# Gate and up of a SwiGLU half as a 2x2 block product in seven half products instead of eight

## The chip, the cores and the metric

One core of one Trainium2 chip runs the whole layer in one program. The metric is device microseconds of one execution, as the median over runs. The core has a matrix engine (TensorE, "PE" in the profile, with its weight loads shown apart as "PEld"), VectorE ("DVE"), ScalarE ("ACT"), GpSimd ("POOL") and a queue that issues the transfers from device memory ("SP"). Each engine works through its own instructions in the order in which they stand, and waits for the others through semaphores. TensorE's operands lie in SBUF; its results lie in PSUM, in banks of 128 partitions by 512 numbers.

## The reference

The layer is a SwiGLU half, a mixing stage and a second SwiGLU half, all in float32, for 512 tokens of width 1024 and a hidden width of 2816.

```python
def rms_norm(x, g, eps=RMS_EPS):
    xf = x.astype(jnp.float32)
    ms = jnp.mean(xf * xf, axis=-1, keepdims=True)
    return (xf * lax.rsqrt(ms + eps) * g.astype(jnp.float32)).astype(x.dtype)

def swiglu(x, w_gate, w_up, w_down):
    return (jax.nn.silu(x @ w_gate) * (x @ w_up)) @ w_down
...
        x = x + FFN_HALF * swiglu(rms_norm(x, norm_ffn1[l]), ffn1_gate[l], ffn1_up[l], ffn1_down[l])
        ...
        x = x + jnp.concatenate([o_sb, o_rw], axis=-1) @ w_out[l]
        x = x + FFN_HALF * swiglu(rms_norm(x, norm_ffn2[l]), ffn2_gate[l], ffn2_up[l], ffn2_down[l])
```

## The kernel before

Everything is kept transposed: a tile has 128 features in the partitions and the 512 tokens along the free axis. `X` is the layer's state in 8 such tiles. A SwiGLU half (`ffn`) runs over `NF` = 22 feature tiles of 128 hidden features. For each it forms gate and up as products over 8 k tiles (`dense`, `gemm`), then `t` = gate times the norm scale `S`, a Silu of it on ACT, `u` = up times `S`, and their product `h` on POOL. The `S` of a half is ready only after its first gate product, since the norm's weight `g` goes into the input tiles and its scale comes in behind the product. After the 22 tiles come 8 down products over all of them ("dn"), which add into `X`.

Each float32 product is made of three passes. Both operands are split into a high part `hi` (rounded to float32r) and a low part `lo` = value minus `hi`; `mm3` (lines 176 to 179) multiplies high by high, high by low and low by high. The weights are split as they arrive (`load_split`): line 162 is the rounding on ACT, line 163 the subtraction on VectorE, both of whose operands lie in SBUF:

```python
        cp(hi[:, :n], raw[:, :n])
        pool.tensor_tensor(lo[:, :n], raw[:, :n], hi[:, :n].bitcast(F32), SUB)
```

So a feature tile takes 4 weight blocks of 128 by 512, 4 roundings on ACT, 4 subtractions on VectorE, and 2 x 8 x 3 = 48 matmuls of 128x512. `h` is split in the same way (lines 189, 190) and kept for the down products. POOL has one instruction per feature tile, line 302.

A scheduler places the instructions of each engine from the program's order and from priorities; `tc.high_priority(500)` moves an instruction forward. The result is fixed at build time. Tiles of a tag share a fixed number of buffers (`NB`): a new one waits until the last reader of the one before is done.

Of the kernel before, what the change touches and what calls it, by code (L numbers as in the profile page):

```python
# [24 lines left out]
P = 128  # L25
T = 512
# [56 lines left out]
def layer(ctx, tc, a, out, dbg=None):  # L83
# [15 lines left out]
    NW = 3  # L99

    def slot(tag, s="t", dt=F32, shape=None):
        return pb.tile(shape or [P, T], dt, tag="s" + tag, name=nm(s), bufs=NB[tag])
# [11 lines left out]
        return ap.rearrange("p (c f) -> p c f", f=f)  # L114


    X = [pc.tile([P, T], F32, name=f"x{k}") for k in range(KD)]
# [27 lines left out]
    def v(n, j=0):  # L145
        return vec[:, VEC[n] + j:VEC[n] + j + 1]
# [7 lines left out]
    def load_split(src, n, s="w", pool=None, cp=nc.scalar.copy):
        if pool is None:
            wct[0] += 1
            pool = nc.gpsimd if mixing[0] and wct[0] % 2 else nc.vector
# [6 lines left out]
        return hi, lo  # L164

    mms = []
    sp = []
# [5 lines left out]
                follow(ins, mms[n - KD])  # L173


    def mm3(ps, lh, ll, rh, rl, start, stop):
        mms.append(nc.tensor.matmul(ps, lhsT=lh, rhs=rh, start=start, stop=False))  # L177
        nc.tensor.matmul(ps, lhsT=lh, rhs=rl, start=False, stop=False)  # L178
        nc.tensor.matmul(ps, lhsT=ll, rhs=rh, start=False, stop=stop)  # L179

    def split(src, tag, scale=None, s="o"):
        if tag in "qb":
# [11 lines left out]
        return hi, lo  # L194


    def norm_in(g):
        return [split(X[k], "x", v(g, k), "x") for k in range(KD)]

    def head_sum(ps, x):  # L200

# [31 lines left out]
        E = spread(ms, RMS_EPS) if want_e else None  # L233
        return S, rs, E

    def gemm(ps, wsrc, xs):
# [9 lines left out]
    def dense(wsrc, xs, s):  # L246
        ps = bank("acc", s)
        gemm(ps, wsrc, xs)
        return ps


    def ffn(g, wgu, wd, last):
        S = None
        if last:
            xs = norm_in(g)
            first = None
        else:
            xs = []

            def first():  # L260
# [17 lines left out]
                nc.sync.dma_start(lev, a["lev"])  # L278
                return ps
        hid = []  # L280
        home = ["q"] * NB["q"] + ["b"] * NB["b"] + [t_ for t_ in "ivkgr" for _ in range((NB[t_] - 2 * (t_ == "r")) // 2)]
        for f in range(NF):
            if f == 0 and first:
                pg, pu = first()
            else:
                pg = dense(wgu[2 * f], xs, "g")
                if f == 1 and first:
                    hold(5)
            if S is None:
                S, _, _ = norm_scale(eng=nc.vector if first else nc.gpsimd)  # L290
            if f or not first:
                pu = dense(wgu[2 * f + 1], xs, "u")
                if f == 0:
                    hold(5)
            t = slot("a", "t")
# [580 lines left out]
```

## Time and profile before

| | |
|---|---|
| median of 3 runs (1133.03 to 1138.6) | 1138.26 us |
| the profiled execution's own time | 1135.56 us |
| its span from first to last instruction | 1133.8 us |
| first half, feature tiles 2 to 21 | 31.70 to 249.31 us |
| first half, down products | 249.31 to 369 us |
| second half, feature tiles 2 to 21 | 792.57 to 1010.17 us |
| PE busy, share of the span | 98% |

The profiled execution is the one whose rows are shown; 1.8 us of its time lie outside its span. Busy time of PE is that of pipelined matmuls whose ends are modelled, so the distance between their starts says more than their duration.

### The profile page before, as it was taken

The numbers are of one execution on the slowest core, as the hardware profiler recorded it, in microseconds if no ns is written. First come the engines' busy times: TensorE is split into PE (matmuls) and PEld (weight loads), VectorE is DVE, ScalarE is ACT, GpSimd is POOL, SyncE is SP. The second block draws the span as 40 slices with busy tenths as digits, with TensorE's granted clock in tenths as the row PEclk, the third lists the DMA queues.
The fourth block names the chain that finished last, engine by engine and source line by source line (L and its number), as shares of the span: only waits on it lengthen the run. The fifth ranks groups of instructions, "written<-read, shape, count | busy, mean of one in ns | idle before, by whom it ended". The sixth has DMA issues, their size and how long they took to land.

```text
span 1133.8 us, 16807 instructions
## 1 busy us (share of the span) xinstructions
PE 1105.7 (98%) x6499; PEld 870.7 (77%) x6499; DVE 567.3 (50%) x966; ACT 445.6 (39%) x782; POOL 182.6 (16%) x135
## 2 busy tenths in 40 slices
PE   8999999999999998999999998999999999999998
PEld 6888888888888766866677665777888888888887
DVE  7444443443333466487777777674434444433322
ACT  6333333333323553364644654553333333322221
POOL 1111111120001233221311312041111111110000
PEclk9999999999999999999999999998999999999999
DMA  5332333233333224311302102022333232334442
GB/s 203 100 96 93 102 93 102 93 90 102 99 93 104 90 66 112 88 47 40 75 27 53 39 23 57 11 74 93 93 101 96 94 102 93 103 90 116 115 114 68
DMA packets 67231, 97.79 MB, mean 86 GB/s; under 512 B 19280, under 2 KB 21456, under 8 KB 67152
## 3 DMA queue, kind: packets, MB, share of 16 engines
q1 hardware_dynamic: 67152, 96.73, 29.0%
q8 instruction: 51, 0.84, 0.3%
q14 instruction: 28, 0.23, 0.1%
HBM read 93.03 MB, written 3.67 MB: 85 GB/s over the span
## 4 chain that ended last, share of the span: by engine, by line
PE 87%; DVE 8%; ACT 2%; issue 1%; DMA 1%; SPq 0%; DVEq 0%; ACTq 0%
PE g L179 7%; PE g L178 7%; PE g L177 7%; PE dn L178 7%; PE dn L177 7%; PE u L179 7%; PE dn L179 7%; PE u L177 7%; PE u L178 7%; PE inv L566 2%; PE z L691 2%; PE o L717 1%; PE k L177 1%; PE k L179 1%; PE k L178 1%
## 5 line engine op out<-in xcount | busy, mean ns | idle before, releaser
L162 ACT CAST wh<-w 128x512 fp32r<-128x512 f32 (+1 forms) x315 | 192.1, 610 | 412.9 <-PE dn L178 146.6
L163 DVE TENSOR_TENSOR wl<-w,wh 128x512 fp32r<-128x512 f32 (+1 forms) x294 | 200.2, 681 | 246.4 <-ACT wh L162 245.7
L179 PE MATMUL g<-xh,wl 128*128 128x512 f32 x352 | 138.1, 392 | 1.9 <-DVE wl L163 1.9
L177 PE MATMUL u<-xh,wh 128*128 128x512 f32 x352 | 137.2, 390 | 2.6 <-ACT wh L162 2.6
L178 PE MATMUL g<-xl,wh 128*128 128x512 f32 x352 | 138.1, 392 | 0.7 <-DVE xl L193 0.7
L177 PE MATMUL g<-xh,wh 128*128 128x512 f32 x352 | 138.2, 393 | 0.1
L179 PE MATMUL u<-xh,wl 128*128 128x512 f32 x352 | 137.1, 390 | 0.0
L178 PE MATMUL u<-xl,wh 128*128 128x512 f32 x352 | 137.1, 389 | 0.0
L302 POOL TENSOR_TENSOR h<-sg,u 128x512 f32<-128x512 f32 x44 | 69.1, 1571 | 395.8 <-DVE u L300 386.2
L177 PE MATMUL dn<-hdh,wh 128*128 128x512 f32 x240 | 93.4, 389 | 0.0
L178 PE MATMUL dn<-hdl,wh 128*128 128x512 f32 x240 | 93.4, 389 | 0.0
L179 PE MATMUL dn<-hdh,wl 128*128 128x512 f32 x240 | 93.4, 389 | 0.0
L179 PEld LDWEIGHTS g<-xh,wl 128*128 128x128 f32 x352 | 66.8, 190 | 16.2 <-DVE wl L163 2.3
L177 PEld LDWEIGHTS u<-xh,wh 128*128 128x128 f32 x352 | 66.1, 188 | 17.1 <-ACT wh L162 3.3
L178 PEld LDWEIGHTS g<-xl,wh 128*128 128x128 f32 x352 | 66.6, 189 | 15.0 <-DVE xl L193 1.1
L177 PEld LDWEIGHTS g<-xh,wh 128*128 128x128 f32 x352 | 66.7, 189 | 14.7 <-ACT sq L134 0.5
L178 PEld LDWEIGHTS u<-xl,wh 128*128 128x128 f32 x352 | 66.2, 188 | 13.7
L179 PEld LDWEIGHTS u<-xh,wl 128*128 128x128 f32 x352 | 66.1, 188 | 13.6
L300 DVE TENSOR_TENSOR u<-u,S 128x512 f32<-128x512 f32 x44 | 30.4, 691 | 65.7 <-PE u L179 65.7
L163 POOL TENSOR_TENSOR wl<-w,wh 128x512 fp32r<-128x512 f32 x22 | 30.4, 1384 | 137.6 <-ACT wh L162 102.6
L177 PEld LDWEIGHTS dn<-hdh,wh 128*128 128x128 f32 x240 | 45.1, 188 | 9.4
L179 PEld LDWEIGHTS dn<-hdh,wl 128*128 128x128 f32 x240 | 45.1, 188 | 9.3
(268 smaller groups left out, 1798.6 us busy)
## 6 DMA issues: line engine op xcount, KB each, us to landing
w<-wgu SPq DMA_DIRECT2D x176, 256.0 KB, 2.6
w<-wd SPq DMA_DIRECT2D x80, 256.0 KB, 2.6
w<-wrw SPq DMA_DIRECT2D x28, 256.0 KB, 2.6
w<-wqk SPq DMA_DIRECT2D x16, 256.0 KB, 2.6
wv<-wv SPq DMA_DIRECT2D x16, 256.0 KB, 2.6
wo<-wo SPq DMA_DIRECT2D x16, 256.0 KB, 2.6
x<-xT SPq DMA_DIRECT2D x8, 256.0 KB, 5.4
w<-wd SPq DMA_DIRECT2D x16, 128.0 KB, 2.0
```

The lines of the kernel that those rows point to most:

```text
L162: cp(hi[:, :n], raw[:, :n])
L163: pool.tensor_tensor(lo[:, :n], raw[:, :n], hi[:, :n].bitcast(F32), SUB)
L177: mms.append(nc.tensor.matmul(ps, lhsT=lh, rhs=rh, start=start, stop=False))
L178: nc.tensor.matmul(ps, lhsT=lh, rhs=rl, start=False, stop=False)
L179: nc.tensor.matmul(ps, lhsT=ll, rhs=rh, start=False, stop=stop)
L300: nc.vector.tensor_tensor(u, pu, S, MUL)
L302: nc.gpsimd.tensor_tensor(h, sg, u, MUL)
L566: nc.tensor.matmul(ps[rows[p], cc], lhsT=l_[rows[p], cc], rhs=r[rows[p], cc], start=True, stop=True)
L691: nc.tensor.matmul(pz[p][:, 0:L], lhsT=qh[rows[p], i * P:L], rhs=kh[rows[p], 0:L], start=True, stop=False)
L717: nc.tensor.matmul(po[rows[p], i * P:L], lhsT=Vt[b][:, hd * CH:(hd + 1) * CH], rhs=ats[p][:, b * P:(b + 1) * P], start=b == 0, stop=b == i)
```

## The change

In each half, feature tiles 0 and 1 stay as they were. For tiles 2 to 21, gate and up over the two halves of k are taken as a 2x2 matrix of blocks (`G1`, `G2` over `U1`, `U2`), the normed input as a 2x2 matrix over halves of k and halves of the tokens. The product of the two takes eight half products (128 features, 4 k tiles, 256 tokens); `seven` makes it of seven, from sums of the weight blocks and of the input blocks (Strassen's method in Winograd's form, with the sign of up turned, which the factor -0.5 at the down product turns back). Each half product is 4 x 3 = 12 matmuls of 128x256 (`mm3s`), 84 per feature tile. Three PSUM banks per tile (`pa`, `pc`, `pe`) collect them, and are read in between.

`halves` makes the seven input operands once per half: it needs `S` first, makes the normed input (`xn`, 8 instructions), four sums (`xy`) and 14 splits (`xch`, `xcl`). Per feature tile, `seven` adds four sums of weight blocks on POOL (`s1` to `s4`, line 326 of the changed kernel), so that seven blocks are split in place of four, and combines the banks in 256-column instructions.

```diff
-    NB = {"x": 16, "q": 3, "b": 4, "r": 10, "i": 10, "c": 6, "v": 4, "k": 4, "g": 8, "a": 4, "t": 2, "f": 4, "s": 2}
+    NB = {"x": 16, "q": 3, "b": 4, "r": 10, "i": 10, "c": 6, "v": 4, "k": 4, "g": 8, "a": 4, "t": 2, "f": 4, "s": 2, "X": 8}
...
+        def blocks(h):
+            t_ = [quad("xn", tag="b") for _ in range(2)]
+            for i in range(2):
+                for q in range(2):
+                    k = 4 * h + 2 * i + q
+                    nc.vector.scalar_tensor_tensor(t_[i][:, q * T:(q + 1) * T], X[k], v(g, k), S, MUL, MUL)
...
+        def parts(m, src):
+            r = []
+            for i in range(2):
+                hi, lo = slot(next(tags), "xch", F32R), slot(next(tags), "xcl", F32R)
+                nc.scalar.copy(c3(hi, HT), src[i])
+                nc.vector.tensor_tensor(c3(lo, HT), src[i], c3(hi, HT).bitcast(F32), SUB)
...
+        y1 = combine(lambda o, i: nc.gpsimd.tensor_tensor(o, b11[i], b12[i], SUB))
+        parts(5, y1)
...
+        y3 = combine(lambda o, i: nc.gpsimd.tensor_tensor(o, b22[i], b12[i], SUB))
+        y6 = combine(lambda o, i: nc.vector.scalar_tensor_tensor(o, y3[i], -1.0, b11[i], MUL, SUB))
...
+        y4 = combine(lambda o, i: nc.vector.scalar_tensor_tensor(o, y6[i], -1.0, b21[i], MUL, SUB))
...
+    def mm3s(ps, w, x, start):
+
+        for k in range(4):
+            ks = slice(k * P, (k + 1) * P)
+            mm3(ps[:, 0:HT], w[0][:, ks], w[1][:, ks], x[k][0], x[k][1], start and k == 0, k == 3, not start)
+
+    def seven(gate, up, need, put):
+
+
+        def sum_split(a_, b_, s):
+            t_ = slot("X", s)
+            nc.gpsimd.tensor_tensor(t_, a_, b_, ADD)
+            hi, lo = slot("X", s + "h", F32R), slot("X", s + "l", F32R)
+            nc.scalar.copy(hi, t_)
+            nc.vector.tensor_tensor(lo, t_, hi.bitcast(F32), SUB)
+            return t_, (hi, lo)
...
+        mm3s(pa, w_split(G1), need(1), True)
+        with tc.high_priority(500):
+            nc.scalar.copy(cu[:, lh], pa[:, lh])
+        yield
+        s1, w = sum_split(U1, U2, "s1")
+        mm3s(pc_, w, need(5), True)
+        with tc.high_priority(500):
+            nc.scalar.copy(h[:, rh], pc_[:, lh])
+        s2, w = sum_split(s1, G1, "s2")
+        mm3s(pa, w, need(6), False)
+        with tc.high_priority(500):
+            nc.scalar.copy(cu[:, rh], pa[:, lh])
+        G2 = raw("s", gate[:, k2], "wg")
+        mm3s(pe, w_split(G2), need(2), True)
+        with tc.high_priority(500):
+            nc.vector.tensor_tensor(cu[:, lh], pe[:, lh], cu[:, lh], ADD)
+        yield
+        _, w = sum_split(G1, U1, "s3")
+        mm3s(pa, w, need(7), False)
+        with tc.high_priority(500):
+            nc.vector.tensor_tensor(h[:, rh], pa[:, lh], h[:, rh], ADD)
+        _, w = sum_split(G2, s2, "s4")
+        mm3s(pc_, w, need(3), False)
+        with tc.high_priority(500):
+            nc.vector.tensor_tensor(cu[:, rh], pc_[:, lh], cu[:, rh], ADD)
+        act(cu, cu, AF.Silu)
+        nc.gpsimd.tensor_tensor(h[:, rh], h[:, rh], cu[:, rh], MUL)
+        mm3s(pa, w_split(U2), need(4), False)
+        nc.vector.tensor_tensor(h[:, lh], pa[:, lh], cu[:, lh], MUL)
+        put(h)
...
+        for f in range(NPL, NF):
+            new = seven(wgu[2 * f], wgu[2 * f + 1], need, put)
+            next(new)
+            if old:
+                for _ in old:
+                    pass
+            next(new)
+            old = new
```

In the built program PE's order repeats for each feature tile, here called A, with B the next and C the one after: the half products with s1(A), s2(A), G2(A), then G1(B), then s3(A), s4(A), U2(A). Call them P1(A), P2(A), P3(A), P4(B), P5(A), P6(A), P7(A).

VectorE before, one feature tile in the middle of the first half: `wl` are splits of weight blocks, `t` and `u` take the gate and up banks times `S`, `hd` is the split of `h`.

```order
L163 TENSOR_TENSOR wl_120_582<-w_118_579,wh_119_581 128x512
L296 TENSOR_TENSOR t_121_597<-g_107_523,S_44_255 128x512
L163 TENSOR_TENSOR wl_129_612<-w_127_609,wh_128_611 128x512
L163 TENSOR_TENSOR wl_132_630<-w_130_627,wh_131_629 128x512
L300 TENSOR_TENSOR u_123_601<-u_114_560,S_44_255 128x512
L163 TENSOR_TENSOR wl_136_649<-w_134_646,wh_135_648 128x512
L190 TENSOR_TENSOR hd_125_605<-h_124_603,hd_125_605 128x512
```

VectorE now, one feature tile in steady state. `cu_227`, `h_228`, `pa_224`, `pc_225`, `pe_226` are tile A's; `wl_277` (G2), `s2l_274`, `s3l_290`, `s4l_293` and `wl_295` (U2) are splits for tile B; `wl_287` (G1) and `s1l_299` are for tile C.

```order
L358 TENSOR_TENSOR cu_227_967<-pe_226_966,cu_227_967 128x256
L164 TENSOR_TENSOR wl_277_1233<-wg_275_1230,wh_276_1232 128x512
L164 TENSOR_TENSOR wl_287_1261<-wg_278_1249,wh_286_1260 128x512
L329 TENSOR_TENSOR s2l_274_1214<-s2_272_1211,s2h_273_1213 128x512
L363 TENSOR_TENSOR h_228_968<-pa_224_964,h_228_968 128x256
L367 TENSOR_TENSOR cu_227_967<-pc_225_965,cu_227_967 128x256
L329 TENSOR_TENSOR s3l_290_1280<-s3_288_1277,s3h_289_1279 128x512
L371 TENSOR_TENSOR h_228_968<-pa_224_964,cu_227_967 128x256
L164 TENSOR_TENSOR wl_295_1318<-wu_252_1108,wh_294_1317 128x512
L329 TENSOR_TENSOR s4l_293_1299<-s4_291_1296,s4h_292_1298 128x512
L197 TENSOR_TENSOR hd_268_1189<-h_228_968,hd_268_1189 128x512
L329 TENSOR_TENSOR s1l_299_1340<-s1_297_1337,s1h_298_1339 128x512
```

Eight of these twelve subtract two operands in SBUF (7 weight splits and `hd`); the four 256-column ones read a bank. The reading of `pa_224` in line 363, which P7(A) waits for, stands behind the splits of B's G2, C's G1 and B's s2.

POOL now, the same stretch (before, its only instruction per tile was `h`, line 302): B's s2 and s3, the product `h` of A, B's s4, and C's s1.

```order
L326 TENSOR_TENSOR s2_272_1211<-s1_269_1192,wg_250_1104 128x512
L326 TENSOR_TENSOR s3_288_1277<-wg_250_1104,wu_251_1106 128x512
L369 TENSOR_TENSOR h_228_968<-h_228_968,cu_227_967 128x256
L326 TENSOR_TENSOR s4_291_1296<-wg_275_1230,s2_272_1211 128x512
L326 TENSOR_TENSOR s1_297_1337<-wu_279_1251,wu_280_1253 128x512
```

The product `h` of A, which needs A's Silu, now stands ahead of B's s4 and C's s1.

ACT now, the same stretch, with B's sums rounded (line 328), weight blocks G2 of B and G1 of C rounded (line 163), and A's Silu (line 135).

```order
L328 CAST s2h_273_1213<-s2_272_1211 128x512
L163 CAST wh_276_1232<-wg_275_1230 128x512
L163 CAST wh_286_1260<-wg_278_1249 128x512
L345 COPY cu_256_1113<-pa_253_1110 128x256
L328 CAST s3h_289_1279<-s3_288_1277 128x512
L135 ACTIVATE cu_227_967<-cu_227_967 128x512
```

The rounding of B's G2 stands behind that of B's s2, and so behind the sum on POOL; the Silu of A stands behind the rounding of B's s3.

## Rows read from the trace of the kernel before

**Rows 1.** Page, part 1: engine, busy us (share of the span) xinstructions.

```profile
PE 1105.7 (98%) x6499; PEld 870.7 (77%) x6499; DVE 567.3 (50%) x966; ACT 445.6 (39%) x782; POOL 182.6 (16%) x135
```

**Rows 2.** Tiles 2 to 21: busy of PE, PEld, DVE, ACT, POOL; clock, DMA.

```profile
31.70:249.31 217.61, 217.61 (x962) 180.24 (x961) 91.39 (x140) 72.83 (x120) 31.48 (x20) 1.00 0.31 97
...
792.57:1010.20 217.63, 217.63 (x962) 180.27 (x961) 91.39 (x140) 72.86 (x121) 31.45 (x20) 1.00 0.31 97
```

**Rows 3.** Timeline of PE, feature tile 17: start us, us, engine, line, operation.

```profile
200.12 0.39 PE L179 MATMUL g<-xh,wl 128*128 128x512 f32 x1
200.34 0.39 PE L177 MATMUL u<-xh,wh 128*128 128x512 f32 x1
```

**Rows 4.** Timeline of PE's weight loads, at 19 and 200 us.

```profile
19.36 0.86 PEld L215 LDWEIGHTS ms<-ones,sq 128*128 128x128 f32 x7
...
200.12 0.19 PEld L177 LDWEIGHTS u<-xh,wh 128*128 128x128 f32 x1
```

**Rows 5.** Instructions grouped by shape: count, busy us, mean ns, idle before.

```profile
L162 ACT CAST wh<-w 128x512 fp32r<-128x512 f32 x299 | 185.5, 621 | 379.6 <-PE u L178 138.9 <-PE dn L178 113.4 <-PE g L178 77.1
L134 ACT ACTIVATE sg<-t 128x512 f32<-128x512 f32 x44 | 27.8, 633 | 15.6 <-DVE t L296 15.6
...
L703 DVE TENSOR_TENSOR r<-z,l 128x256 f32<-128x256 f32 x8 | 3.3, 415 | 0.1
```

**Rows 6.** Timeline of DVE, around two POOL products.

```profile
26.69 0.69 DVE L296 TENSOR_TENSOR t<-g,S 128x512 f32<-128x512 f32 x1
27.30 1.28 DVE L163 TENSOR_TENSOR wl<-w,wh 128x512 fp32r<-128x512 f32 x1
...
43.39 0.68 DVE L163 TENSOR_TENSOR wl<-w,wh 128x512 fp32r<-128x512 f32 x1
```

**Rows 7.** Timeline of POOL, the same two stretches.

```profile
26.74 1.29 POOL L302 TENSOR_TENSOR h<-sg,u 128x512 f32<-128x512 f32 x1 [4.75 <-ACT sg L134]
...
43.65 1.57 POOL L302 TENSOR_TENSOR h<-sg,u 128x512 f32<-128x512 f32 x1 [9.31 <-DVE u L300]
```

**Rows 8.** Timeline of DVE and of POOL, 757 to 767 us.

```profile
757.82 0.68 DVE L747 TENSOR_TENSOR x<-wo,x 128x512 f32<-128x512 f32 x1
758.42 0.74 DVE L193 SCALAR_TENSOR_TENSOR xl<-x,vec,xh 128x512 fp32r<-128x512 f32 x1
759.08 0.68 DVE L747 TENSOR_TENSOR x<-wo,x 128x512 f32<-128x512 f32 x1
...
758.65 8.40 POOL L212 TENSOR_TENSOR sq<-sq,sq 128x512 f32<-128x512 f32 x5 [1.31 <-ACT sq L134]
```

**Rows 9.** Timeline of ACT at 506 us: two instructions back to back.

```profile
506.13 0.63 ACT L134 ACTIVATE Pd<-Gs 128x512 f32<-128x512 f32 x1
506.66 0.62 ACT L134 ACTIVATE Pi<-Gs 128x512 f32<-128x512 f32 x1
```

**Rows 10.** POOL: a full-width difference, and the narrowest one (min/median/max ns).

```profile
L163 POOL TENSOR_TENSOR wol<-wo,woh 128x512 fp32r<-128x512 f32 x8 | 10.3, 1287 | 77.0 <-ACT woh L162 62.8 <-DVE H L538 8.1 <-ACT l L134 6.1
...
L435 POOL TENSOR_SCALAR PC<-Pd x4: 248/729/732, 418.8 to 626.4; 128x8 f32<-128x8 f32 x4
```

**Rows 11.** Timeline of DVE: the norm scale S of each half, first use.

```profile
24.57 0.69 DVE L229 TENSOR_SCALAR S<-sp 128x512 f32<-128x512 f32 x1 [0.22 <-PE sp L226]
25.30 0.69 DVE L296 TENSOR_TENSOR t<-g,S 128x512 f32<-128x512 f32 x1
...
779.97 0.69 DVE L229 TENSOR_SCALAR S<-sp 128x512 f32<-128x512 f32 x1 [0.18 <-PE sp L226]
```

**Rows 12.** Timeline of PE: first matmul of each half's down projection.

```profile
249.31 0.39 PE L177 MATMUL dn<-hd,wh 128*128 128x512 f32 x1
...
1010.17 0.39 PE L177 MATMUL dn<-hd,wh 128*128 128x512 f32 x1
```

**Rows 13.** Start of the second half: the same columns as Rows 2.

```profile
763.00:768.00 5.00, 1.94 (x6) 0.94 (x6) 5.00 (x6) 2.90 (x5) 3.90 (x3) 0.80 0.02 3
768.00:774.00 6.00, 6.00 (x17) 4.70 (x17) 2.77 (x5) 0.62 (x1) 0.00 (x0) 0.60 0.40 131
```

More of the change, by code (lines that the diff above doesn't have):

```diff
@@ L114, in c3 @@
         return ap.rearrange("p (c f) -> p c f", f=f)
-    X = [pc.tile([P, T], F32, name=f"x{k}") for k in range(KD)]
+    X = [slot("X", "x") for _ in range(KD)]
     vec = pc.tile([P, NVEC], F32, name="vec")
@@ L152, in layer, with load, w_split @@
     wct = [0]
[L154 to L157, printed above, removed]
+    def load(src, n, s="w"):
         raw = pw.tile([P, T], F32, tag="raw", name=nm(s), bufs=NW)
         nc.sync.dma_start(raw[:, :n], src)
+        return raw
+    def w_split(raw, n=T, s="w", pool=nc.vector, cp=nc.scalar.copy):
         hi = pw.tile([P, T], F32R, tag="whi", name=nm(s + "h"), bufs=NW)
@@ L164, in load_split @@
         return hi, lo
+    def load_split(src, n, s="w", pool=None, cp=nc.scalar.copy):
+        if pool is None:
+            wct[0] += 1
+            pool = nc.gpsimd if mixing[0] and wct[0] % 2 else nc.vector
+        return w_split(load(src, n, s), n, s, pool, cp)
     mms = []
@@ L194, in split, with norm_in @@
         return hi, lo
-    def norm_in(g):
-        return [split(X[k], "x", v(g, k), "x") for k in range(KD)]
+    def norm_in(g, tags="x" * KD):
+        return [split(X[k], tags[k], v(g, k), "x") for k in range(KD)]
     def head_sum(ps, x):
@@ L234, in norm_scale, with gemm @@
         return S, rs, E
-    def gemm(ps, wsrc, xs):
+    def gemm(ps, wsrc, xs, step=lambda: None):
         n = len(xs)
@@ L252, in ffn @@
     def ffn(g, wgu, wd, last):
         S = None
+        xsrc = a["xT"]
         if last:
-            xs = norm_in(g)
+            xsrc = pd.tile([KD, P, T], F32, name="xmid")
+            for k in range(KD):
+                nc.sync.dma_start(xsrc[k], X[k])
+            xs = norm_in(g, XTAG)
             first = None
@@ L280, in ffn, with put, step, need @@
         hid = []
-        home = ["q"] * NB["q"] + ["b"] * NB["b"] + [t_ for t_ in "ivkgr" for _ in range((NB[t_] - 2 * (t_ == "r")) // 2)]
-        for f in range(NF):
+        home = ["v"] * 2 + ["r"] * 4 + ["q"] * 3 + ["b"] * 4 + ["i"] * 5 + ["g"] * 4
+        def put(h):
+            hid.append(split(h, home[len(hid)], None, "hd"))
+        made = {}
+        hv = [None]
+        def step():
+            if hv[0]:
+                made.update(next(hv[0], made))
+        def need(m):
+            while m not in made:
+                step()
+            return made[m]
+        for f in range(NPL):
             if f == 0 and first:
@@ L285, in ffn @@
             else:
-                pg = dense(wgu[2 * f], xs, "g")
+                pg = dense(wgu[2 * f], xs, "g", step)
                 if f == 1 and first:
@@ L291, in ffn @@
             if f or not first:
-                pu = dense(wgu[2 * f + 1], xs, "u")
+                pu = dense(wgu[2 * f + 1], xs, "u", step)
                 if f == 0:
                     hold(5)
+            if f == 0:
+                hv[0] = halves(g, S)
             t = slot("a", "t")
@@ L299, in ffn @@
             u = slot("a", "u")
-            nc.vector.tensor_tensor(u, pu, S, MUL)
+            nc.vector.scalar_tensor_tensor(u, pu, -1.0, S, MUL, MUL)
             h = slot("a", "h")
             nc.gpsimd.tensor_tensor(h, sg, u, MUL)
-            hid.append(split(h, home[f] if f < len(home) else "a", None, "hd"))
+            put(h)
+        old = None
+        for f in range(NPL, NF):
[6 more added lines that the diff above has]
+            old = new
+        for _ in old:
+            pass
         for m in range(KD):
+            X[m] = slot("X", "x")
+            nc.sync.dma_start(X[m], xsrc[m])
             ps = dense(wd[m], hid, "dn")
```

59 lines of the change are left out of this document (50 added, 9 removed).

## The prediction

> **What bounds the kernel now.** The page's busy shares come first: PE is busy for 98% of the span; apart from its own weight loads nothing is busy for more than 50% [rows 1]. Over feature tiles 2 to 21 of a half, PE is busy for all of the 217.6 us [rows 2]: 20 tiles of 48 matmuls, 960 matmuls, 226.7 ns each, 10.88 us a tile. The timeline shows the same step, 0.22 to 0.23 us from one start to the next [rows 3]. In this stretch the other engines have air: per tile VectorE is busy for 91.39 / 20 = 4.6 us, ACT 3.6, POOL 1.6 [rows 2]. Transfers take a DMA share of 0.31, and the change loads the same four weight blocks per tile. So the question is whether PE's work shrinks, and whether the rest, which grows, still fits beside it.
>
> **PE's own work.** 48 matmuls of 512 columns become 84 of 256. No row shows such a matmul. If the step were proportional to columns, it would be 113 ns. A full step is 226.7 ns, of which 512 columns at the granted 2.4 GHz are 213.3 ns; if the other 13 ns are paid per matmul, 256 columns take 120 ns. Each matmul also has its own weight load. Seven loads in a row take 0.86 us, the last one 0.19 of it, so one follows the other by (0.86 - 0.19) / 6 = 111 ns; and a load starts together with the matmul ahead of it, so it lies under it [rows 3, 4]. That is close to the limit but just inside it. I take 120 ns, between 113 (proportional) and 227 (no gain from fewer columns). A half product is then 12 x 0.120 = 1.44 us and a tile 7 x 1.44 = 10.08, which is 0.80 less than 10.88. Over 40 tiles that would be -32 us, if nothing else ended later than PE.
>
> The Trainium skill has a rule that speaks against this: "TensorE: Matmul & The Clock Gate", section "The mechanism", says that a weight load overlaps a running matmul only when the two use different row groups. By it, load and matmul would add up, and a tile would take 84 x (0.111 + 0.113) = 18.8 us. The rows here disagree: at 512 columns the step would be 0.213 + 0.111, and it is 0.227. The rest of the sum does not use this rule; it returns among the rivals.
>
> **What collides.** POOL's work grows from one instruction per tile to four sums and a half-width product; VectorE's from 5 subtractions of SBUF operands to 8. A difference of two SBUF tiles on POOL takes 1.29 us by itself [rows 10]. Now see what the two engines do to each other. At 26.74 POOL starts a product of 1.29 us; VectorE's split begins at 27.30 while it runs and takes 1.28 in place of 0.68, ending 0.55 behind it. The other way round, a split starts at 43.39, POOL's product at 43.65, and the product takes 1.57 [rows 6, 7]. The instruction `t` at 26.69, which reads one operand from PSUM, lies under the same product and keeps its 0.69 [rows 6]. So a POOL instruction and a VectorE instruction with two SBUF operands exclude each other for most of their length. Five in a row show the price: POOL's sums follow each other by 8.40 / 5 = 1.68 us while VectorE puts one such instruction between each two [rows 8]. I take 1.68 us for a pair. Bounds: 1.29, if VectorE's part were hidden, and 1.29 + 0.68 = 1.97, if nothing overlapped. The change makes nearly every one of POOL's instructions meet such a one.
>
> The Trainium skill names this: "SBUF — State Buffer", section "Who interferes with whom", says that whichever starts first holds the shared port for the whole instruction while the other blocks fully. The rows agree on who blocks, but not on the length: by the page a pair is 1.97 us, by the rows 1.68.
>
> **The ring.** With these durations I follow the order of VectorE, POOL and ACT from one reading of `pa` after P5 (line 363, tile A) to the next (tile B). A VectorE instruction follows the one ahead after 0.60 to 0.61 us at 512 columns, its last 0.08 being covered [rows 8]; a 256-column one of 0.415 [rows 5] after 0.33. On ACT, 0.62 becomes 0.53 back to back [rows 5, 9]. A hand-over between instructions costs 0.04 (24.57 + 0.69 to 25.30) [rows 11]. A half-width POOL product lies between 0.25 (narrowest) and 1.29, linearly 0.77 [rows 10].
> 1. Reading `pa` 0.33; reading `pc` into `cu` and hand-over 0.455; Silu 0.633 + 0.04 [rows 5]; POOL's half product 0.73: together 2.19.
> 2. POOL s4(B), s1(C), s2(C), each with one split between them (U2(B), s4(B), `hd`(A)): 3 x 1.68 = 5.04.
> 3. Split of s1(C) and hand-over 0.65; ACT rounds s2(C) 0.53 and G2(C) 0.66; split of G2(C) 0.61: 2.45.
> 4. Split of the following tile's G1, which meets POOL's s3(C): 1.68. Split of s2(C): 0.61. Then the next reading of `pa`.
>
> The sum is 2.19 + 5.04 + 2.45 + 2.29 = 11.97, say 12.0 us per tile. Behind the reading of `pa` waits P7, and behind P7 all of PE, so PE then stands still for some 2 us in each tile. The ring does not contain P1 to P7: another matmul duration between 113 and 143 ns (12.0 / 84) leaves it as it is. ACT's work of at most 12 x 0.62 = 7.4 us and VectorE's of 8 x 0.68 + 4 x 0.415 = 7.1 us would each fit in 10 us; it is the order with the collisions that doesn't.
>
> **The start of each half.** The seven input operands need `S`, which is there at 25.3 us (24.57 + 0.69) and at 780.7 [rows 11]. From there to the first split of tile 3's s1, VectorE has 43 instructions: 26 of `halves` (8 `xn`, 14 `xcl`, 4 `xy`), 6 of tiles 0 and 1, 9 weight splits, 2 bank readings. 25 differences at 0.61, 12 scaled ones at 0.66 (758.42 to 759.08 [rows 8]), 4 and 2 readings at 0.61 and 0.33: 26.3 us. POOL has 11 instructions in between, and each adds 1.68 - 0.66 = 1.02: 11.2. Some of them fall under bank readings, so I take 36 us together, between 26.3 and 37.5. PE, which has dense work of tile 1 for only 6.4 us behind `S` in the first half and 11.9 in the second (31.70 and 792.57 [rows 2]), waits.
>
> From the split of tile 3's s1 there are 18 rings to that of tile 21, and from there 4.74 (the ring's end) + 0.48 (reading of `pa`) + 7 x 1.44 = 15.3 us to the down products. First half: 25.3 + 36 + 18 x 12.0 + 15.3 = 292.6, against 249.3 before [rows 12]: +43.3. Second: 780.7 + 36 + 216 + 15.3 = 1048.0, against 1010.2: +37.8. The down products stay as they are: their splits run as before, and the 24 added transfers of the state (8 out, 16 in) lie under 120 us of matmuls at a DMA share of about a third. In the mixing stage VectorE, ACT and PE have the same order. The sum is +81 us on the profiled execution's 1135.6: 1217 us. That execution is 2.7 us under the median of the runs, 0.2%, well inside what I call no change, 0.5%.
>
> **Rivals.**
> - *Collisions cost nothing, and PE stays the bound* (0.13). Without them the ring is 2.19 + 3 x 1.29 + 0.04 + 0.53 + 0.66 + 3 x 0.61 = 9.1, below 10.08, and the start is 26.3 us. First half: 25.3 + 26.3 + 18 x 10.08 + 6 x 1.44 = 241.7 (-7.6); second 997.1 (-13.1): 1115 us, faster. For it: `t` and `u` show VectorE working under POOL unhindered. Against: rows 6 to 8. It decides if a pair costs under 1.29 us.
> - *The ring is shorter, about 11 us* (0.11): a collision of the four falls beside a wait that is there anyway. 36 tiles less 1 us: 1180.
> - *The clock falls* (0.10). After 5 us in which PE worked for 1.94, the granted clock was 0.60 for the next 6 us [rows 13], which is time at 1.2 GHz. If the 2 us pause of each tile did this, P7 and P1(B) behind it would take about twice their 2.88 us, and s1(C) waits for P1(B)'s buffer. It has only 0.3 us in hand: its turn in the ring comes 3.87 us after the reading of `pa`, and P1(B) ends after 0.48 + 2.88 + 0.2. So up to 2.3 us per tile: 1217 + 36 x 2.3 = 1300. Against: the clock came back while PE was busy, and here it works for 10 of 12 us.
> - *Full-length exclusion, as the page on SBUF has it* (0.03): four pairs of 1.97, 13.2 us per tile, 1217 + 36 x 1.2 = 1260.
> - *Weight loads don't overlap, as the page on TensorE has it* (0.02): 18.8 - 10.88 = +7.9 us for 40 tiles: 1450.
>
> **How the numbers follow.** The ring as it stands has 0.61 of the chance; a pair between 1.55 and 1.80 us and a start between 30 and 38 make it 1190 to 1245. I predict its 1217. The range takes in most of the 11-us ring and the page's longer lock: 1170 to 1262; outside lie the fast rival and most of the slow clock, about 0.2. Faster by over 0.5% is the first rival: 0.14. Between it and the short ring little lies, 0.03 for no change. Slower: 0.83.
>
> **What would show it.** Right: tiles 2 to 21 at about 12 us; one pause of PE per tile, ahead of the U2 product, ended by the reading of `pa` in line 363; splits of 1.2 to 1.8 us on VectorE, or sums of over 1.5 on POOL; and PE nearly idle for over 15 us behind `S`. Wrong: a tile near 10 us with PE busy throughout (then the exclusion does not hold for these sums), matmuls of 256 columns at 143 ns or more, or a granted clock below 0.9 in the tiles.

## The result, and the profile after

The changed kernel takes 1238.69 us (median of 4 runs, 1237.15 to 1241.85), the kernel before 1136.89 us on the same chip. The ratio is 1.0904, with a 95% interval of 1.0867 to 1.0942: slower by 102 us. The forecast was 1217 us, between 1170 and 1262, so the direction and the range held, and the change of 102 us was forecast as 81, 21 us short. The profiled execution took 1241.85 us, its span 1240.0.

Part 1 of the page of the changed kernel answers to [rows 1]: engine, busy us, share of the span, instructions.

```profile
PE 1122.8 (91%) x7939; PEld 948.5 (76%) x7939; DVE 824.4 (66%) x1218; ACT 561.0 (45%) x1050; POOL 408.7 (33%) x303
```

VectorE has 257 us more to do than before and POOL 226 us more; PE's share falls from 98% to 91%. The windows of the changed kernel show where. The first and third stretch run from S to the split of tile 4's s1, the second and fourth from there to that of tile 21's, 17 tiles each; columns as in [rows 2].

```profile
25.86:72.01 46.15, 30.00 (x176) 26.30 (x176) 43.45 (x53) 22.42 (x43) 26.14 (x17) 0.82 0.24 74
72.01:286.56 214.55, 184.13 (x1414) 180.68 (x1414) 168.97 (x206) 103.58 (x204) 117.36 (x87) 0.94 0.25 82
836.73:886.12 49.39, 38.74 (x201) 33.37 (x201) 44.10 (x56) 24.12 (x45) 26.41 (x17) 0.83 0.26 80
886.12:1099.43 213.31, 183.74 (x1424) 180.29 (x1423) 171.80 (x205) 103.61 (x204) 116.79 (x86) 0.95 0.25 81
```

A tile takes 214.55 / 17 = 12.62 and 213.31 / 17 = 12.55 us, against 10.88 before, and PE is busy for 184.13 / 17 = 10.83 and 183.74 / 17 = 10.81 of them. In front of these tiles stand 46 and 49 us in which VectorE is busy for 43.45 and 44.10 us, and PE for 30.00 and 38.74.

Now the costliest groups of the page: line, engine, operation, tiles, count, then busy us and mean ns of one, then the idle time of the engine just before them and what ended it.

```profile
L184 PE MATMUL pa<-xch,wh 128*128 128x256 f32 x320 | 99.9, 312 | 71.2 <-DVE h L363 64.3
L164 DVE TENSOR_TENSOR wl<-wg,wh 128x512 fp32r<-128x512 f32 x80 | 85.8, 1108 | 33.1 <-ACT wh L163 33.1
L326 POOL TENSOR_TENSOR s<-wg,wu 128x512 f32<-128x512 f32 x40 | 65.7, 1641 | 94.8 <-PE pa L186 83.6
L326 POOL TENSOR_TENSOR s<-s,wg 128x512 f32<-128x512 f32 x40 | 64.0, 1600 | 5.5 <-POOL s L326 2.2
L329 DVE TENSOR_TENSOR s4l<-s,s4h 128x512 fp32r<-128x512 f32 x40 | 49.5, 1237 | 17.3 <-PE pc L185 9.1
```

PE's pauses are where they were forecast: 64.3 us of idle time end with the reading of `pa` in line 363, ahead of the U2 product. The two groups of POOL's sums in these rows take 1.6 us in place of the 1.29 of [rows 10], and the two of VectorE's splits 1.1 to 1.2 us on average, in place of 0.68.

One tile on VectorE, from one reading of `pa` to the next (timeline: start us, us, then the instruction, then the idle time before it):

```profile
216.72 0.41 DVE L363 TENSOR_TENSOR h<-pa,h 128x256 f32<-128x256 f32 x1
217.06 0.41 DVE L367 TENSOR_TENSOR cu<-pc,cu 128x256 f32<-128x256 f32 x1
217.39 0.67 DVE L329 TENSOR_TENSOR s3l<-s,s3h 128x512 fp32r<-128x512 f32 x1
218.99 0.42 DVE L371 TENSOR_TENSOR h<-pa,cu 128x256 f32<-128x256 f32 x1 [0.93 <-PE pa L186]
219.45 1.30 DVE L164 TENSOR_TENSOR wl<-wu,wh 128x512 fp32r<-128x512 f32 x1
220.89 1.56 DVE L329 TENSOR_TENSOR s4l<-s,s4h 128x512 fp32r<-128x512 f32 x1
222.37 1.78 DVE L197 TENSOR_TENSOR hdl<-h,hdh 128x512 fp32r<-128x512 f32 x1
224.08 0.68 DVE L329 TENSOR_TENSOR s1l<-s,s1h 128x512 fp32r<-128x512 f32 x1
224.68 0.41 DVE L358 TENSOR_TENSOR cu<-pe,cu 128x256 f32<-128x256 f32 x1
226.02 2.39 DVE L164 TENSOR_TENSOR wl<-wg,wh 128x512 fp32r<-128x512 f32 x2 [0.93 <-ACT wh L163]
228.33 0.68 DVE L329 TENSOR_TENSOR s2l<-s,s2h 128x512 fp32r<-128x512 f32 x1
228.93 0.41 DVE L363 TENSOR_TENSOR h<-pa,h 128x256 f32<-128x256 f32 x1
```

And POOL in the same tile:

```profile
218.21 0.74 POOL L369 TENSOR_TENSOR h<-h,cu 128x256 f32<-128x256 f32 x1 [2.56 <-ACT cu L135]
218.90 1.29 POOL L326 TENSOR_TENSOR s<-wg,s 128x512 f32<-128x512 f32 x1
220.40 1.50 POOL L326 TENSOR_TENSOR s<-wu,wu 128x512 f32<-128x512 f32 x1 [0.20 <-PE pc L186]
221.98 1.63 POOL L326 TENSOR_TENSOR s<-s,wg 128x512 f32<-128x512 f32 x1
226.16 1.69 POOL L326 TENSOR_TENSOR s<-wg,wu 128x512 f32<-128x512 f32 x1 [2.55 <-PE pa L186]
```

This tile takes 228.93 - 216.72 = 12.21 us. Read the two side by side: the split of U2 (219.45) meets POOL's sum for s4, the split of s4 its sum for s1, that of `hd` its sum for s2, and the second of the two weight splits at 226.02 its sum for s3. The splits that meet nothing, s1l, s2l and s3l, keep their 0.67 to 0.68 us, and the instructions that read a bank of PSUM keep their 0.41.

Not every tile is like this one: some are a good microsecond longer. Windows of the tile before the one shown and of its surroundings, same columns; the granted clock stands third from the end.

```profile
202.20:203.84 1.64, 0.00 (x1) 0.01 (x1) 1.64 (x4) 0.62 (x1) 0.10 (x1) 1.00 0.29 64
203.84:205.20 1.36, 1.36 (x10) 1.36 (x11) 0.87 (x2) 0.63 (x1) 0.34 (x1) 0.85 0.83 298
205.20:208.30 3.10, 3.10 (x16) 3.10 (x16) 1.24 (x2) 1.75 (x3) 1.62 (x2) 0.52 0.14 30
208.30:214.00 5.70, 5.70 (x50) 5.70 (x49) 4.47 (x5) 2.63 (x6) 3.37 (x2) 1.00 0.22 78
214.00:217.20 3.20, 1.69 (x15) 1.48 (x14) 3.20 (x5) 1.19 (x3) 1.33 (x1) 1.00 0.13 31
217.20:226.30 9.10, 9.10 (x76) 9.10 (x77) 7.07 (x9) 5.01 (x10) 5.26 (x5) 1.00 0.31 107
```

After the pause that ends at 203.84 PE works without a break, and for 3.1 us of that at a mean granted clock of 0.52 of full speed, so nearly all of it at 1.2 GHz: 16 matmuls start in 3.10 us, against 50 in 5.70 us at 2.4 GHz. From one reading of `pa` to the next it is 13.3 us here. The pause before 217.20 is followed by no such drop.

The down products begin at 302.94 and 1116.41 us, against 249.31 and 1010.17 [rows 12]:

```profile
302.94 0.40 PE L184 MATMUL dn<-hdh,wh 128*128 128x512 f32 x1
...
1116.41 0.40 PE L184 MATMUL dn<-hdh,wh 128*128 128x512 f32 x1
```

### The profile page after: what moved, and what is told of

Read it like the earlier page. It is cut to its first block, busy times and chain, and to the rows that moved or that the text cites. A ratio compares the mean times of both kernels' runs of the same rounds, so it can differ in the third digit from the quotient of the medians.

```text
span 1240.0 us, 20591 instructions
## 1 busy us (share of the span) xinstructions
PE 1122.8 (91%) x7939; PEld 948.5 (76%) x7939; DVE 824.4 (66%) x1218; ACT 561.0 (45%) x1050; POOL 408.7 (33%) x303
## 4 chain that ended last, share of the span: by engine, by line
PE 60%; DVE 19%; issue 10%; POOL 5%; ACT 4%; DMA 1%; SPq 0%; DVEq 0%; POOLq 0%; ACTq 0%
PE dn L185 6%; PE dn L186 6%; PE dn L184 6%; POOL s L326 4%; PE pa L184 4%; PE pa L186 3%; PE pa L185 3%; DVE wl L164 3%; PE inv L725 2%; DVE xcl L283 2%; PE z L850 2%; DVE s1l L329 1%; PE pc L186 1%; PE pc L184 1%; PE pc L185 1%
## 5 line engine op out<-in xcount | busy, mean ns | idle before, releaser
L164 DVE TENSOR_TENSOR wl<-w,wh 128x512 fp32r<-128x512 f32 x134 | 92.6, 691 | 171.4 <-ACT wh L163 170.2
L163 ACT CAST wh<-w 128x512 fp32r<-128x512 f32 (+1 forms) x155 | 92.7, 598 | 218.8 <-PE dn L185 150.7
L184 PE MATMUL pa<-xch,wh 128*128 128x256 f32 x320 | 99.9, 312 | 71.2 <-DVE h L363 64.3
L184 PEld LDWEIGHTS pa<-xch,wh 128*128 128x128 f32 x320 | 65.3, 204 | 79.7 <-DVE h L363 70.7
L164 DVE TENSOR_TENSOR wl<-wg,wh 128x512 fp32r<-128x512 f32 x80 | 85.8, 1108 | 33.1 <-ACT wh L163 33.1
L186 PE MATMUL pa<-xch,wl 128*128 128x256 f32 x320 | 96.6, 302 | 2.2 <-DVE wl L164 2.1
L326 POOL TENSOR_TENSOR s<-wg,wu 128x512 f32<-128x512 f32 x40 | 65.7, 1641 | 94.8 <-PE pa L186 83.6
L185 PE MATMUL pa<-xcl,wh 128*128 128x256 f32 x320 | 95.8, 299 | 0.0
L186 PEld LDWEIGHTS pa<-xch,wl 128*128 128x128 f32 x320 | 66.4, 207 | 3.2 <-DVE wl L164 3.2
L185 PEld LDWEIGHTS pa<-xcl,wh 128*128 128x128 f32 x320 | 66.3, 207 | 0.3 <-DVE xcl L283 0.3
L329 DVE TENSOR_TENSOR s4l<-s,s4h 128x512 fp32r<-128x512 f32 x40 | 49.5, 1237 | 17.3 <-PE pc L185 9.1
```

The lines of the kernel that those rows point to most:

```text
L326: nc.gpsimd.tensor_tensor(t_, a_, b_, ADD)
L329: nc.vector.tensor_tensor(lo, t_, hi.bitcast(F32), SUB)
```

## The experiments

The theory: POOL's sums and VectorE's instructions with two SBUF operands exclude each other, this stretches the queue of VectorE to 12.2 us per tile, and PE waits for it; drops of the clock add to it. The rivals: PE itself is slower at 256 columns; it is the waiting for POOL's long results and not the exclusion; the drops come by themselves; the start of a half is paced by PE. The first seven kernels are edits of the changed kernel, the last four build on each other. A tile's time is the distance between two readings of `pa`. A time without a range is that of a single run, so a few microseconds between two of these prove nothing by themselves (the runs of the changed kernel lie 4.7 us apart).

**The sums on VectorE.**

```diff
-            nc.gpsimd.tensor_tensor(t_, a_, b_, ADD)
+            nc.vector.tensor_tensor(t_, a_, b_, ADD)
```

> The four sums of a tile run on VectorE, the rest as it is. Theory (the sums on POOL and VectorE's instructions with two SBUF operands exclude each other, and the order behind them makes the ring): VectorE has 12 x 0.61 + 4 x 0.415 = 9.0 us of work per tile and one collision left, with the product of h; PE is the bound at 10.1 to 10.6 us per tile, and the kernel takes 1130 to 1180 us. Rival (PE is slower at 256 columns for reasons of its own, clock included): a tile stays over 11.5 us, 1200 us or more.

Measured: 1160.64 us (4 runs, 1157.2 to 1161.4), ratio to the kernel before 1.0214 (1.0185 to 1.0244). A tile takes 10.58 us:

```profile
103.70:251.80 148.10, 148.10 (x1178) 142.61 (x1177) 127.54 (x225) 84.85 (x168) 13.92 (x14) 1.00 0.31 97
```

These are 14 tiles. The sums take 0.68 to 0.71 us each on VectorE, and 78 of the 102 us are gone. VectorE has four more instructions per tile and is busy for less of it, 127.54 / 14 = 9.11 us against 168.97 / 17 = 9.94 in the changed kernel. The 0.5 us over PE's own 10.08 are two short waits of PE in each tile, for the split of s2 and the rounding of s4.

**No sums.**

```diff
-            t_ = slot("X", s)
-            nc.gpsimd.tensor_tensor(t_, a_, b_, ADD)
+            t_ = a_
```

> The four sums are left out, and the first operand of each is split in its place; the output is therefore another one. Theory: POOL's only work in a tile is the product of h, the ring is gone, and PE is the bound at 10.1 us per tile; with a start of some 30 us the kernel takes 1120 to 1145 us. Rival (something other than the sums holds the tile): over 11.5 us per tile, 1200 us or more.

Measured: 1130.75 us. PE is busy for all of 17 tiles at 171.30 / 17 = 10.08 us, which is 84 x 120.0 ns:

```profile
66.30:237.60 171.30, 171.30 (x1430) 171.30 (x1429) 122.79 (x204) 108.32 (x205) 14.06 (x18) 1.00 0.30 101
```

So 256-column matmuls cost PE nothing extra, and the whole surplus of the tiles hangs on the sums. It also shows how little there is to win: even without any sums this run is only 5 us faster than the kernel before (1135.86 us, the median of 7 runs beside it), since the start of each half remains.

**The sums on VectorE, and again on POOL for nobody.** This one separates exclusion from waiting.

```diff
-            nc.gpsimd.tensor_tensor(t_, a_, b_, ADD)
+            nc.vector.tensor_tensor(t_, a_, b_, ADD)
+            nc.gpsimd.tensor_tensor(spare[0], a_, b_, ADD)
...
+        spare[0] = slot("r", "spare")
```

> As with the sums on VectorE, but POOL computes the same four sums a second time into a spare tile that nobody reads. Theory of collisions: the tile is lengthened though nothing waits for POOL's results, by up to 4 x 1.07 us, to 12 to 14 us; 1210 to 1290 us. Rival (what costs is that ACT and VectorE wait for POOL's long sums, not that they lock each other out): the same time as with the sums on VectorE alone, within 10 us.

Measured: 1295.71 us, 135 us more than without the spare sums; a tile takes 13.85 us where no clock drop disturbs it, 3.3 us more. A window of 14 tiles, drops included, columns as before:

```profile
122.30:319.10 196.80, 162.82 (x1177) 150.83 (x1176) 176.38 (x226) 86.67 (x168) 102.91 (x70) 0.97 0.24 74
```

Groups of VectorE, first the kernel without the spare sums, then this one:

```profile
L329 DVE TENSOR_TENSOR s2l<-s,s2h 128x512 fp32r<-128x512 f32 x40 | 27.6, 690 | 0.0
L326 DVE TENSOR_TENSOR s<-s,wg 128x512 f32<-128x512 f32 x40 | 27.6, 690 | 0.0
```

```profile
L332 DVE TENSOR_TENSOR s2l<-s,s2h 128x512 fp32r<-128x512 f32 x40 | 69.9, 1748 | 0.0
L328 DVE TENSOR_TENSOR s<-s,wg 128x512 f32<-128x512 f32 x40 | 67.5, 1686 | 0.0
```

Nothing reads the spare tile, and VectorE's instructions still become 1 us longer each, where they meet one, without idle time ahead of them. So exclusion alone lengthens a tile by 3.3 us, and it is what lengthens the splits that meet a sum in the rows of the changed kernel; the rival that expected the time of the first experiment falls.

**Filling the pause.** 14 matmuls into a free bank between P6 and P7 keep PE at work:

```diff
+        z, x4 = bank("sd", "z"), need(4)
+        for j in range(14):
+            fill = nc.tensor.matmul(z[:, 0:HT], lhsT=x4[0][0][:, 0:P], rhs=x4[0][0], start=j == 0, stop=j == 13)
+            follow(fill, mms[-1])
...
+        follow(mms[-4], fill)
```

> 14 matmuls of 256 columns into a bank that nobody reads stand between P6 and P7 of each tile, 1.7 us in the pause of about 2 us. Theory (the pause drops the clock in about every third tile, and that costs the ring about 0.45 us on average): the 3.4 us stretches at 0.5 go away, every tile takes 12.2 us, and the kernel 1215 to 1230 us. Rival 1 (the drops come by themselves, whatever PE does): they stay, 1235 to 1245. Rival 2 (the filling delays P7): tiles over 12.5 us without drops, 1240 or more.

Measured: 1279.9 us, 13.48 us per tile at a clock of 1.00 in the tiles. The drops were gone, and yet the tile was longer, as the second rival has it. But the scheduler had also changed VectorE's order: the split of `hd` now came ahead of that of s4. The run therefore doesn't show what the filling itself costs, and the next one holds the order of the changed kernel.

**Filling the pause, with the order held.** The same, and in `split`, `sum_split` and `w_split`:

```diff
+                    follow(hdl.pop(), ins)
...
+            follow(s4h.pop(), cast)
```

> The same 14 filling matmuls between P6 and P7, but VectorE and ACT are held to the order of the changed kernel (in the run before, VectorE took the split of hd ahead of that of s4, and a tile took 13.48 us at full clock). Theory (the drops of the clock come from the pause and cost 0.35 to 0.5 us per tile on average; the other 0.2 us over the forecast are durations): full clock, every tile 12.2 us, 1218 to 1230 us. Rival (the filling itself lengthens the tile, whatever the order): over 12.8 us per tile again, 1250 us or more.

Measured: 1236.07 us. The tiles take 12.23 us, at a clock of 1.00; the two stretches below are 16 and 17 tiles long:

```profile
93.10:288.90 195.80, 192.21 (x1570) 188.97 (x1569) 162.19 (x194) 97.77 (x192) 110.58 (x81) 1.00 0.24 84
890.40:1098.30 207.90, 204.41 (x1670) 200.96 (x1668) 173.38 (x206) 103.87 (x204) 116.17 (x85) 1.00 0.24 83
```

With the pause filled the drops are gone, so they come from the pause, and without them a tile is 0.32 to 0.39 us shorter than the 12.55 and 12.62 of the changed kernel. The total came down by 3 us only, not by the 9 to 21 expected, and 3 us are within the spread of the runs. The traces show one loss: the filling stands in the first tiles too, and from the first to the second reading of `pa` it is now 19.4 us in place of 15.4 in the first half, 18.5 in place of 17.3 in the second. Against the run before it, the order of VectorE's and ACT's instructions alone is worth 13.48 - 12.23 = 1.25 us per tile.

**The product of h on VectorE**, the sums still on POOL.

```diff
-        nc.gpsimd.tensor_tensor(h[:, rh], h[:, rh], cu[:, rh], MUL)
+        nc.vector.tensor_tensor(h[:, rh], h[:, rh], cu[:, rh], MUL)
```

> The half-width product of h runs on VectorE, the four sums stay on POOL. Theory of the ring (POOL's sum for s4 waits behind that product, the product for Silu, and Silu for the reading of pa): the 2.19 us step leaves the ring, what is left is VectorE's own queue of 4 x 1.68 + 4 x 0.61 + 5 x 0.415 = 11.2 us per tile, and the kernel takes 1185 to 1205 us. Rival (only the sum of the collisions counts, the order on POOL does not): VectorE has 0.415 us more to do, 12.3 us or more per tile, 1240 to 1260 us.

Measured: 1237.7 us, 12.11 us per tile between clock drops. The expected microsecond did not come, nor did the 1240 us or more of the rival. VectorE's timeline and POOL's show why:

```profile
180.36 1.56 DVE L369 TENSOR_TENSOR h<-h,cu 128x256 f32<-128x256 f32 x1
...
188.13 2.39 DVE L164 TENSOR_TENSOR wl<-wg,wh 128x512 fp32r<-128x512 f32 x2 [0.93 <-ACT wh L163]
```

```profile
180.34 1.30 POOL L326 TENSOR_TENSOR s<-wg,s 128x512 f32<-128x512 f32 x1 [2.49 <-DVE s3l L329]
```

POOL's sum for s4 does start earlier, 1.42 us behind the reading of `pa` (at 178.92) in place of 2.18. But it now meets the product itself, 0.02 us ahead of it, and that half-width instruction takes 1.56 us. VectorE has four collisions in a tile as before, and the wait of 0.93 us for ACT, which the expected 11.2 us had left out. By these rows the way through Silu and POOL's product was one of two that are about equally long; without it VectorE's own queue, with its collisions and that wait, sets 12.1 us.

**Three plain tiles instead of two in each half.**

```diff
-    NPL = 2
+    NPL = 3
```

> Three feature tiles of each half are computed in the plain way instead of two (19 by half products). Theory (from S to the split of tile 3's s1 VectorE and POOL set the pace, PE waits): per half one ring of 12.6 us less, and some 4.6 us of VectorE's work for a plain tile more, 8 us less per half, 1215 to 1230 us. Rival (PE's own chain sets the start, so that a plain tile of 10.9 us covers waiting time one for one): 20 us or more less per half, under 1200 us.

Measured: 1233.4 us. From S to the down products 273.2 and 276.0 us, against 277.1 and 279.7: 3.9 and 3.7 us less. That is half of what the theory gave, and why only half stays open; it is far from the rival's 20 us, so PE's own chain does not set the start. In the changed kernel, of the PE waits that the trace lists from S to the split of tile 4's s1, 13.0 of 16.3 us in the first half and 8.3 of 10.5 in the second end with an instruction of VectorE, the others with one of ACT.

**Nothing of a tile on POOL, and four plain tiles.** Both edits above (sums and product of h on VectorE), and:

```diff
-    NPL = 2
+    NPL = 4
```

> Sums and the product of h on VectorE, nothing of a tile left on POOL, and four plain tiles in each half. Theory: no collisions in the tiles, VectorE has 12 x 0.61 + 5 x 0.415 = 9.4 us per tile, PE is the bound at 10.1 to 10.3 us; the plain tiles cover most of the start. Against the kernel before, 18 tiles of a half save up to 0.8 us each: 1108 to 1130 us, faster than before. Rival (the chain of sum, rounding and split through VectorE and ACT holds PE up as with the sums on VectorE alone, 10.6 us per tile, and the start still costs 10 us): 1140 us or more.

Measured: 1140.31 us (10 runs, 1137.78 to 1141.65), ratio 1.0026 (1.0012 to 1.004): no change by the 0.5% bound. The tiles are at 10.08 us, as the theory has it; the time is the rival's. What the tiles win is lost at the start. Windows of two stretches behind S (27.12 us), and 15 tiles:

```profile
33.00:42.00 9.00, 0.75 (x4) 0.29 (x2) 9.00 (x12) 3.97 (x7) 4.33 (x3) 0.82 0.00 1
42.00:52.00 10.00, 7.50 (x16) 5.06 (x17) 9.44 (x15) 4.41 (x9) 2.18 (x2) 0.50 0.16 52
91.60:242.60 151.00, 150.84 (x1257) 150.63 (x1256) 137.30 (x256) 92.24 (x180) 0.00 (x0) 1.00 0.31 102
```

PE stands still for almost 9 us, and the 10 us behind that pass at 1.2 GHz. VectorE is busy throughout the 9 us, and its timeline says what PE waits for:

```profile
41.42 0.68 DVE L442 TENSOR_TENSOR t<-g,S 128x512 f32<-128x512 f32 x1
...
43.87 0.68 DVE L446 SCALAR_TENSOR_TENSOR u<-u,S 128x512 f32<-128x512 f32 x1
```

PE's next matmuls, into banks `g` and `u` of the third plain tile, start at 42.24 and 44.70, just behind the ends of these two: the reading of the second tile's banks stood behind the preparation of the token halves. (The profile puts the first of the two waits down to an `xch` of ACT that ends beside `t`; a matmul of a plain tile doesn't read it.)

**A paced start.** Four plain tiles; the preparation is held back, a few instructions behind each weight split, and `y` and the plain tiles' product are on VectorE too.

```diff
+        need(3)
+        for i, op in enumerate(hv_ops):
+            k = 7 + max(0, i - 2) * 3 // 8
+            if k < len(wl):
+                follow(op, wl[k])
...
```

> The version with four plain tiles and nothing of a half-product tile on POOL; now the preparation of the token halves on VectorE is held behind the weight splits of the plain tiles (about eight of its instructions to three splits), and the differences y and the plain products of h are on VectorE too. In the version before, PE stood still for about 9 us behind S in the first half (no matmul starts between 33.4 and 42.2 us), and ran at half clock until 52 us, because the weight splits were queued behind that preparation. Theory: with the splits in time PE keeps working and keeps its clock; a half then takes 4 x 10.88 + 18 x 10.08 = 225.0 us instead of 22 x 10.88 = 239.4: 1108 to 1122 us, 1.5 to 2.5% faster than the kernel before. Rival (VectorE hasn't the time: 26 instructions of preparation with the plain tiles' own work take longer than the plain tiles, so that PE waits later instead, at the first half products): 1128 us or more.

Measured: 1128.4 us (1124.16 to 1130.07), ratio 0.9924 (0.9906 to 0.9943), 0.8% faster than the kernel before. The pause at 33 us is gone. (The expectation named the weight splits as what PE waited for; by the rows above the 9 us ended with the readings of the banks, which the edit moves forward as well. A weight split ended only a later wait of 0.99 us, at 46.88.) The edit paces the preparation and takes the differences `y` and the plain products off POOL at the same time; how the 12 us divide between the two is not shown. The time is just inside the rival's range, and its reason held in part: from 40 to 60 us VectorE has no pause left and PE still has, and the 15 tiles of the second window take 10.45 us each:

```profile
40.00:60.00 20.00, 17.34 (x79) 13.25 (x77) 20.00 (x34) 12.29 (x21) 0.00 (x0) 1.00 0.24 80
78.30:235.10 156.80, 156.80 (x1262) 152.81 (x1262) 136.93 (x257) 90.25 (x180) 0.00 (x0) 1.00 0.31 99
```

**The same with five plain tiles.** `NPL = 5`, nothing else.

> The same with five plain tiles in each half. Theory (four are enough to hide the preparation): each plain tile costs 0.8 us more than one by half products, 1.6 us in all, so 0 to 4 us slower than with four. Rival (with four VectorE is still late at the first half products): the fifth covers it, 4 us or more faster than with four.

Measured: 1113.52 us (1110.53 to 1116.38), ratio 0.9791 (0.9766 to 0.9817): 2.1% faster than the kernel before, and 15 us faster than with four, a size that the rival allows. But some 30 tiles at 10.08 in place of 10.45 us make 11 of the 13.6 us between the two profiled executions, so most of the gain lies in the tiles and not, as the rival has it, in the start. Windows of the same stretches behind S (25.64 us), and 15 tiles:

```profile
33.00:42.00 9.00, 8.93 (x39) 7.01 (x38) 9.00 (x16) 3.94 (x8) 0.00 (x0) 1.00 0.27 87
42.00:52.00 10.00, 10.00 (x45) 7.80 (x44) 10.00 (x17) 6.84 (x12) 0.00 (x0) 1.00 0.33 106
75.10:226.30 151.20, 151.20 (x1262) 151.20 (x1262) 137.25 (x256) 91.71 (x180) 0.00 (x0) 1.00 0.32 102
```

PE works through the start at full clock, and the tiles are at 10.08. Why the tiles settled at 10.45 with four plain tiles and at 10.08 with five stays open. The number of plain tiles alone does not decide it, since the version without pacing has four and tiles of 10.08. The scheduler put VectorE's instructions in a different order each time, and no run varied that order alone.

**The sums back on POOL** in the version with five plain tiles.

```diff
-            nc.vector.tensor_tensor(t_, a_, b_, ADD)
+            nc.gpsimd.tensor_tensor(t_, a_, b_, ADD)
```

> The version with five plain tiles and a paced start, with one thing undone: the four sums of a tile are on POOL again. Theory (most of the loss of the changed kernel lies in its tiles, from these sums): 34 tiles go from 10.08 back to the 12.5 us that they took on average with the product of h on VectorE, +82 us: 1185 to 1205 us. Rival (the tiles were long because VectorE and PE entered them late, from the crowded start): the tiles stay below 11 us, under 1150 us.

Measured: 1196.48 us, 83 us more; a tile takes 12.11 us, about every third 13.4. The window is 14 tiles long, 12.51 us each:

```profile
94.70:269.90 175.20, 152.12 (x1176) 149.28 (x1176) 155.44 (x184) 86.68 (x168) 83.05 (x56) 0.95 0.26 82
```

The tiles are long with an orderly start too. This one choice of engine is worth 83 us here and 78 us in the first experiment, in kernels that differ otherwise: of the 102 us, about four fifths.

## Why the prediction was right, and where it was short

**PE's own work: right.** 256 columns take 120.0 ns, against 226.7 ns for 512, and PE needs 10.08 us per tile, without the sums and in the versions with four and five plain tiles. The Trainium skill, "TensorE: Matmul & The Clock Gate", section "The mechanism", would let a load overlap only a matmul of another row group, which by the forecast's estimate made a tile of 18.8 us; no run here agrees with that.

**What collides: right.** The spare sums show exclusion by itself, and the price of a pair holds: in the tile shown, VectorE's two collided splits from 220.89 on take 224.08 - 220.89 = 3.19 us together, with POOL's two sums from 220.40 to 223.61 beside them, 1.6 us for a pair, against 1.68. The Trainium skill, "SBUF — State Buffer", section "Who interferes with whom", says that a VectorE instruction with two SBUF inputs contends with a GpSimd instruction that reads SBUF; the 690 ns that became 1748 agree. A lock of full length, as that section of the Trainium skill has it, makes 1.29 + 0.68 = 1.97 us for a pair by estimate; the trace doesn't agree with that.

**The ring: right in each step, too short as a mean.** The tile shown follows the four steps of the forecast: from the reading of `pa` to the sum for s4, 218.90 - 216.72 = 2.18 us (forecast 2.19); from there to the split of s1, 5.18 (5.04; POOL waits 0.20 for PE once); to the end of the first weight split, 226.02 + 0.61 - 224.08 = 2.55 (2.45); the rest 2.30 (2.29). That is 12.21 in place of 11.97. Whether another chain is as long, the forecast did not ask; with the product of h on VectorE a tile still took 12.1 us, so one is.

**The clock: the step that failed.** It was a rival with a chance of 0.10 and up to 2.3 us in every tile. In truth both cases came together: the ring as forecast, and a drop behind about every third pause, mostly 1.0 to 1.2 us each. Per tile that is 12.62 - 12.21 = 0.41 and 12.55 - 12.21 = 0.34 us, and the filled pause confirms it with 12.23. The argument that the clock would hold because PE works for 10 of 12 us was wrong. So was the price of the rival, though: a drop came in about every third tile and cost half of its 2.3 us.

**The start: right in its cause, and in its sum by luck.** Forecast were 36 us from S to the split of tile 3's s1 and one ring of 12.0 from there to tile 4's, 48.0; measured are 46.15 and 49.39. The two parts miss in opposite directions. The first part takes 37.44 us in the first half and 39.47 in the second, there beyond the bound of 37.5:

```profile
25.86:63.30 37.44, 22.00 (x111) 18.51 (x111) 34.88 (x42) 18.17 (x34) 19.48 (x12) 0.77 0.18 57
836.73:876.20 39.47, 28.82 (x134) 23.45 (x134) 37.34 (x46) 19.42 (x36) 20.59 (x12) 0.84 0.21 67
```

The second part takes 46.15 - 37.44 = 8.71 and 49.39 - 39.47 = 9.92 us, so it is not a full ring yet. The sign that PE is nearly idle for over 15 us behind S did not come either: to tile 4's split PE lacks 46.15 - 30.00 = 16.15 us in the first half and 49.39 - 38.74 = 10.65 in the second, in waits of at most 3.6 us. That VectorE sets this time agrees with its busy time, 43.45 and 44.10 us, with the third plain tile and with the paced start.

**The sum.** Against the forecast the profiled execution is 25 us longer. S came 0.6 us later in the first half; the starts give -1.9 and +1.4; the 17 rings +10.5 and +9.3 (204 forecast each); the way from tile 21's split to the down products 16.4 and 17.0 in place of 15.3, +2.8 together; the mixing stage with the first down products 533.8 in place of 531.4, +2.4. The sum is 25.1. The rings are 20 of it: some 7 from durations (34 x 0.21) and 13 from the clock. The 2.4 us are not explained, nor are the 2.8; the stretch of the mixing stage took between 530 and 537 us in the experiments.

**The fast rival** (1115 us, if collisions cost nothing) was worked out from PE's 10.08 us and a start of 26.3. The kernel that has neither collisions nor a late start in fact takes 1113.5. That the two figures are so close is chance, since that kernel has 17 tiles of a half by half products and the rival 20.

## What to carry to other kernels

A change that saves matmuls by adding sums moves the work to the elementwise engines: before judging it, count for each tile how many of POOL's instructions will meet a VectorE instruction with two SBUF operands, since here each meeting made a VectorE instruction about 1 us longer, and putting the sums on the busier engine took 78 us off. When PE is the bound, preparation on the engine that also empties PSUM and splits weights should not be queued ahead of those: here it cost PE a wait of almost 9 us and then 10 us at 1.2 GHz. With both mended, the seven half products, in 17 of the 22 tiles of a half, are 2.1% faster than the kernel before, not 9% slower.

## What the runs showed of the hardware

In the tiles of the changed kernel PE pauses once in 12 us, for 1.1 to 2.4 us, and works for the rest. Behind about every third of these pauses the granted clock fell, as to 0.52 in the 3.1 us behind 205.20; behind the others it did not, though many of them are as long, about 1.9 us. With the pause filled by matmuls the clock stayed at 1.00. A half-width VectorE instruction with two SBUF operands (0.42 us alone, in the version with five plain tiles) that starts 0.02 us behind a POOL sum of 1.30 us takes 1.56 us: it loses about as much as a full-width split does, so a short instruction pays as much as a long one.
